# A gated recurrence's inner blocks: full-array matmuls replaced by fp32 matmuls of 32 stationary columns in four strips of PSUM

## The chip, the core and the metric

The kernel runs as one program on one core of a Trainium2 chip. The metric is the time of one execution on the device in microseconds (us). The kernel before has a median of 1879.35 us over 3 runs (1879.05 to 1879.52). TensorE has two clock levels, 1.2 and 2.4 GHz; the profile gives the granted share, and for this kernel it is 1.000.

## The reference, cut to what matters

Two layers of an encoder trunk, each with four branches (sparse attention, retention, a gated recurrence, attention over a memory) between a wide input projection and an output projection. The sequence has 256 positions in chunks of 64, four heads of 128 channels. The change touches the gated recurrence alone:

```
def hgrn2(f, i, q):          # per chunk of 64 positions, per head
    kin = 1.0 - f
    def step(state, inp):
        f_t, k_t, i_t, q_t = inp
        state = f_t[..., None] * state + k_t[..., None] * i_t[..., None, :]
        return state, einsum('bnhd,bnhdv->bnhv', q_t, state)
    ...
```

Unrolled, the output at position t is a sum over earlier positions s of the value i_s times a score: the sum over channels of q_t, kin_s and the product of all gates f between s and t. The kernel computes these scores as matrices of key position by query position, for blocks of 128 x 128 positions, and multiplies them with the values afterwards.

## The kernel before

**The dense work.** TensorE spends nearly all its time on projections (`gemms`, L254). Each fp32 weight is split into a rounded part and a remainder (ScalarE: `whi`, L243; VectorE: `wlo`, L244), and three matmuls (L271 to L273) take the place of one. A weight piece of 256 rows is 12 matmuls of up to 512 moving columns, and is cut four pieces ahead at most (`HL = 4` buffers of each part). All names in rows that begin with `u`, `wo`, `bw`, `mk` and `mv` are such projections.

**The order.** The smaller work of the branches is written as Python generators. After each weight piece `stream.pump` (L127) lets the waiting generators take up to two steps, and what a step issues stands there in each engine's program. `stream.rest(n)` (L106) waits for n pieces and `stream.bank()` (L111) for one of two PSUM tiles. So the order on each engine is fixed when the program is built, and TensorE runs the branch matmuls between projection matmuls.

**The recurrence.** `hgrn_scores` (L553) holds q, kin and the running gate products with channels in partitions and positions along the free axis, 8 groups (4 heads x 2 halves of the sequence) of 128 positions. A score matrix `a` of key positions by query positions is filled from the diagonal outward:

- The diagonal ("own": q times kin) and the positions next to it ("near") are sums over channels: the products are split into two halves (`halves`, L581, an ACT cast and a DVE subtraction for each) and multiplied with a 128 x 128 tile of ones (`summed`, L587; PSUM tiles `cdg` and `cnr`). The sums come out alike in all partitions; a multiplication with an identity and a masked copy take the wanted ones.
- Then three levels, m = 2, 8, 32 (`QUADS`, L615): groups of four blocks of m positions. For each of the 8 groups one fp32 matmul (L637, PSUM tile `cl`) multiplies 128 stationary columns (key positions) with 192 moving columns (the query blocks that are wanted, tile `cV`, made on L624 to L627). Of its output of 128 x 192 only the blocks within each group of four are wanted; masked copies (L642) bring them into `a`. Between the levels `decayed` (L568) multiplies gate products into q and kin.

An fp32 matmul in the program appears in the trace as two passes, each with its own weight load, so `x8` stands for four matmuls. After the levels come the product across the halves (`cx`, L654) and the product with the values (`co`, L528 to L532).

Of the kernel before, what the change touches and what calls it, by code (L numbers as in the profile page):

```python
# [10 lines left out]
F32 = mybir.dt.float32  # L11
F32R = mybir.dt.float32r
U8 = mybir.dt.uint8
# [25 lines left out]
    _o += DM * _n  # L39
assert _o == DM * INW  # L40

C_ID, C_D, C_COS, C_SIN, C_LEV = 0, 128, 128 + 1536, 128 + 1536 + 256, 128 + 1536 + 512
QUADS, FROM = (2, 8, 32), (0, 1, 2, 0, 1, 0)
C_END = C_LEV + 64 + 192 * len(QUADS)


def shape_constants():
    c = np.zeros((128, C_END), np.float32)
    c[:, C_ID:C_ID + 128] = np.eye(128, dtype=np.float32)
    log_g = np.log1p(-np.exp2(-5.0 - np.arange(NH)))  # L50
    t = np.arange(S)
    dist = np.abs(t[None, :] - t[:, None])
    seen = (t[:, None] // CH) <= (t[None, :] // CH)
    dec = np.where(seen[:, None, :], np.exp(log_g[None, :, None] * dist[:, None, :]), 0.0) * ISQ
    c[:, C_D:C_D + 1024] = dec[:128].reshape(128, 1024)
    c[:, C_D + 1024:C_D + 1536] = dec[128:, :, 128:].reshape(128, 512)
    inv = np.float32(10000.0) ** (-np.arange(0, HD, 2, dtype=np.float32) / np.float32(HD))
    ang = t.astype(np.float32)[:, None] * inv[None, :]
    cos, sin = np.cos(ang), np.sin(ang)
    for i in range(2):  # L60
        r = slice(128 * i, 128 * i + 128)
        c[:, C_COS + 128 * i:C_COS + 128 * i + 128] = np.concatenate([cos[r], cos[r]], 1)
        c[:, C_SIN + 128 * i:C_SIN + 128 * i + 128] = np.concatenate([-sin[r], sin[r]], 1)
    s = np.arange(128)
    c[:, C_LEV:C_LEV + 64] = s[:, None] == 2 * np.arange(64)[None, :]
    for i, m in enumerate(QUADS):
        at, block = np.divmod(np.arange(192), 6 * m)
        start = 4 * m * at + m * np.array(FROM)[block // m]
        c[:, C_LEV + 64 + 192 * i:C_LEV + 256 + 192 * i] = (s[:, None] >= start) & (s[:, None] < start + m)
    return c  # L70


# [111 lines left out]
def trunk(ctx: ExitStack, tc: tile.TileContext, x, xt, memt, ng, qkg, hg, lbl, win, wmem, wbr, wout,  # L184
# [23 lines left out]

    xs = cst.tile([128, 2, DM], F32, name="xs")
    csb = cst.tile([128, C_END], F32, name="csb")  # L210
    msb = cst.tile([128, 512 + 192 * len(QUADS)], U8, name="msb")
    ones = cst.tile([128, 128], F32R, name="ones")
# [5 lines left out]
    ident = csb[:, C_ID:C_ID + 128]  # L218
    ve.memset(nhalf, -0.5)

    plan = gemm_plan(wmem, win, wbr, wout)
    stream = Stream()
# [330 lines left out]
    def hgrn_scores(uf, uq, lb, olb, name):  # L553
# [60 lines left out]
        tot = decayed(1, tot)  # L614
        for i, m in enumerate(QUADS):  # L615
            n = 32 // m
            yield
            mask = msb[:, 512 + 192 * i:704 + 192 * i].rearrange("p (n x) -> p n x", n=n)
            vs = []
            for half in range(2):  # L620
                qv = qf[:, 512 * half:512 * half + 512].rearrange("p (n b j) -> p n b j", b=4, j=m)
                dv = tot.rearrange("p (h n b) -> p h n b", h=2, b=4)[:, half]
                vt = G([128, 4 * n, 6, m], f"{name}V{half}")
                ac.copy(vt[:, :, 0:3, :], qv[:, :, 1:4, :])  # L624
                ve.tensor_mul(vt[:, :, 3:5, :], qv[:, :, 2:4, :],
                              dv[:, :, 1:3, None].to_broadcast([128, 4 * n, 2, m]))
                ve.tensor_mul(vt[:, :, 5, :], vt[:, :, 4, :], dv[:, :, 1:2].to_broadcast([128, 4 * n, m]))  # L627
                vs.append(vt.rearrange("p (g n) b j -> p g (n b j)", g=4))
            yield
            yield from stream.rest(1)  # L630
            for half in range(2):
                yield
# [6 lines left out]
                pv = ps[:, :, :192].rearrange("p g (n x) -> p g n x", n=n)  # L639
                av = a[:, 4 * half:4 * half + 4, :].rearrange("p g (n x) -> p g n x", n=n)  # L640
                for t0, at, w in ((1, 0, 3), (2, 3, 2), (3, 5, 1)):
                    ve.copy_predicated(av[:, :, :, t0 * m:],  # L642
                                       mask[:, None, :, at * m:(at + w) * m].to_broadcast([128, 4, n, w * m]),
                                       pv[:, :, :, at * m:(at + w) * m])
                stream.free()
            yield
            tot = decayed(m, tot)
            yield
            tot = decayed(2 * m, tot)
        yield from stream.rest(3)  # L650
        yield from stream.bank()
        ps = PB(name + "x")[:, :512].rearrange("p (h t) -> p h t", h=4)
# [79 lines left out]
    def last_constants():  # L732
        yield from stream.rest(27)
        sy.dma_start(csb[:, C_D:], cf[:, C_D:])
        yield from stream.rest(7)
        po.tensor_copy(msb[:, :512].rearrange("p (g t) -> p g t", g=8),
                       csb[:, C_LEV:C_LEV + 64][:, None, :].to_broadcast([128, 8, 64]))
        po.tensor_copy(msb[:, 512:], csb[:, C_LEV + 64:C_END])
        one = G([128, 128], "one")
        ve.memset(one, 1.0)  # L740
        ac.copy(ones, one)
        lower_bounds()

    lbv = cst.tile([128, L, NH], F32, name="lbv")
# [197 lines left out]
```

## Time and profile before

| | |
|---|---|
| median of 3 runs | 1879.35 us (1879.05 to 1879.52) |
| profiled execution, its own time | 1878.9 us |
| its span, first to last instruction | 1877.1 us |
| TensorE (PE) busy | 1869.4 us, 8574 passes |
| VectorE (DVE) busy | 1153.6 us |
| ScalarE (ACT) busy | 872.8 us |
| GpSimd (POOL) busy | 252.8 us |
| granted TensorE clock | 1.000 |

A pass's busy time in the profile holds its way through the array, which overlaps the next pass. What a pass costs TensorE is the step from its start to the next one's start. `PEld` is TensorE's weight load, which is issued by the same sequencer.

### The profile page before, as it was taken

The page shows a single profiled execution, that of the slowest core. Times are in us where ns is not written, and L with a number is a line of the kernel's source. Part 1 is how long each engine was busy: PE and PEld are TensorE (multiplying, and loading weights), DVE is VectorE, ACT ScalarE, POOL GpSimd, SP SyncE. Part 2 cuts the span into 40 slices and gives each one's busy share as a digit, 9 for nine tenths or more (in the row PEclk, how much of TensorE's full clock was granted, in tenths as well). Part 3 has the DMA queues.
Part 4 walks back from the last instruction along what each step waited for, and adds up shares of the span by engine and source line. Part 5 has one row for each costly group of instructions (what it writes and reads, how often), then busy time and mean ns, then how long its engine had stood idle before and what let it go on. Part 6 is the DMA issues. An engine that isn't in the chain of part 4 may idle for free.

```text
span 1877.1 us, 22921 instructions
## 1 busy us (share of the span) xinstructions
PE 1869.4 (100%) x8574; PEld 1560.4 (83%) x8574; DVE 1153.6 (61%) x1269; ACT 872.8 (46%) x1013; POOL 252.8 (13%) x404
## 2 busy tenths in 40 slices
PE   9999999999999999999999999999999999999999
PEld 7888888888888888888888888888888888888887
DVE  6645788675655555555566578867565555555554
ACT  5654445544444444444455454553444444444442
POOL 0301032241200000000021103224120000000000
PEclk9999999999999999999999999999999999999999
DMA  9865656677756565565686565768765656556563
GB/s 347 287 215 163 218 173 202 215 197 188 218 188 211 190 203 202 185 208 196 199 233 213 168 219 172 207 199 208 194 204 202 197 196 209 187 200 201 189 209 116
DMA packets 165662, 381.39 MB, mean 203 GB/s; under 512 B 111792, under 2 KB 112688, under 8 KB 124720
## 3 DMA queue, kind: packets, MB, share of 16 engines
q1 hardware_dynamic: 153120, 367.86, 60.0%
q0 software_dynamic: 12288, 11.95, 3.7%
q8 instruction: 67, 1.10, 0.3%
q14 instruction: 43, 0.35, 0.1%
q10 hardware_dynamic: 144, 0.13, 0.0%
HBM read 353.92 MB, written 2.10 MB: 190 GB/s over the span
## 4 chain that ended last, share of the span: by engine, by line
PE 98%; DMA 1%; DVE 1%; issue 0%; ACT 0%; SPq 0%; DVEq 0%; ACTq 0%
PE u L271 24%; PE u L272 24%; PE u L273 24%; PE wo L272 3%; PE wo L271 3%; PE bw L273 3%; PE bw L272 3%; PE bw L271 3%; PE wo L273 3%; PE cl L637 1%; DMA raw<-in_wmem 1%; PE mk L273 1%; PE mv L272 1%; PE mv L271 1%; PE mv L273 1%; PE mk L272 1%
## 5 line engine op out<-in xcount | busy, mean ns | idle before, releaser
L244 DVE TENSOR_TENSOR wlo<-raw,whi 128x1024 fp32r<-128x1024 f32 (+2 forms) x676 | 803.6, 1193 | 634.3 <-ACT whi L243 630.4
L243 ACT CAST whi<-raw 128x1024 fp32r<-128x1024 f32 (+2 forms) x676 | 695.6, 1031 | 928.5 <-PE u L273 712.4
L322 POOL DMA_DIRECT2D mgp<-mgpi x64 | 36.8, 583 | 798.8 <-ACT whi L243 503.6
L272 PE MATMUL u<-wlo,x10h 128*128 128x512 f32 (+2 forms) x256 | 98.4, 384 | 0.6 <-DVE wlo L244 0.6
L272 PE MATMUL u<-wlo,x00h 128*128 128x512 f32 (+2 forms) x256 | 98.4, 384 | 0.6 <-DVE wlo L244 0.6
L271 PE MATMUL u<-whi,x03h 128*128 128x512 f32 (+2 forms) x256 | 98.9, 386 | 0.0
L271 PE MATMUL u<-whi,x13h 128*128 128x512 f32 (+2 forms) x256 | 98.9, 386 | 0.0
L271 PE MATMUL u<-whi,x00h 128*128 128x512 f32 (+2 forms) x256 | 98.9, 386 | 0.0
L271 PE MATMUL u<-whi,x10h 128*128 128x512 f32 (+2 forms) x256 | 98.9, 386 | 0.0
L271 PE MATMUL u<-whi,x02h 128*128 128x512 f32 (+2 forms) x256 | 98.8, 386 | 0.0
L271 PE MATMUL u<-whi,x12h 128*128 128x512 f32 (+2 forms) x256 | 98.8, 386 | 0.0
L271 PE MATMUL u<-whi,x01h 128*128 128x512 f32 (+2 forms) x256 | 98.7, 386 | 0.0
L271 PE MATMUL u<-whi,x11h 128*128 128x512 f32 (+2 forms) x256 | 98.7, 386 | 0.0
L272 PE MATMUL u<-wlo,x03h 128*128 128x512 f32 (+2 forms) x256 | 98.2, 383 | 0.0
L272 PE MATMUL u<-wlo,x13h 128*128 128x512 f32 (+2 forms) x256 | 98.2, 383 | 0.0
L272 PE MATMUL u<-wlo,x02h 128*128 128x512 f32 (+2 forms) x256 | 98.2, 383 | 0.0
L272 PE MATMUL u<-wlo,x12h 128*128 128x512 f32 (+2 forms) x256 | 98.2, 383 | 0.0
L272 PE MATMUL u<-wlo,x01h 128*128 128x512 f32 (+2 forms) x256 | 98.2, 383 | 0.0
L272 PE MATMUL u<-wlo,x11h 128*128 128x512 f32 (+2 forms) x256 | 98.2, 383 | 0.0
L273 PE MATMUL u<-whi,x00l 128*128 128x512 f32 (+2 forms) x256 | 98.2, 383 | 0.0
L273 PE MATMUL u<-whi,x01l 128*128 128x512 f32 (+2 forms) x256 | 98.1, 383 | 0.0
L273 PE MATMUL u<-whi,x10l 128*128 128x512 f32 (+2 forms) x256 | 98.1, 383 | 0.0
(390 smaller groups left out, 3715.7 us busy)
## 6 DMA issues: line engine op xcount, KB each, us to landing
raw<-in_win SPq DMA_DIRECT2D x240, 1024.0 KB, 4.9
raw<-in_wbr SPq DMA_DIRECT2D x32, 1024.0 KB, 4.8
raw<-in_wout SPq DMA_DIRECT2D x32, 1024.0 KB, 4.9
raw<-in_wmem SPq DMA_DIRECT2D x14, 1024.0 KB, 8.2
raw<-in_win SPq DMA_DIRECT2D x8, 656.0 KB, 4.0
raw<-in_win SPq DMA_DIRECT2D x8, 512.0 KB, 3.5
raw<-in_wmem SPq DMA_DIRECT2D x8, 256.0 KB, 5.7
xr<-in_xt SPq DMA_DIRECT2D x4, 512.0 KB, 8.2
```

What stands on the lines that cost most here:

```text
L243: ac.copy(hi[:, a:b, :], r)
L244: ve.tensor_sub(lo[:, a:b, :], r, hi[:, a:b, :].bitcast(F32))
L271: te.matmul(ps[:, t, :n], ah[:, 2 * j + k, c], wh[:, k, :], start=first, stop=False)
L272: te.matmul(ps[:, t, :n], ah[:, 2 * j + k, c], wl[:, k, :], start=False, stop=False)
L273: te.matmul(ps[:, t, :n], al[:, 2 * j + k, c], wh[:, k, :], start=False, stop=last)
L322: q.dma_start(whole[b, :, a], inner[a, :, b])
L637: te.matmul(ps[:, g, :192], kd[:, h, (g % 2) * 128:(g % 2) * 128 + 128], vs[half][:, g, :], start=True, stop=True)
```

## The change

Only the 32 x 32 blocks on the diagonal of `a` are computed for the diagonal, the neighbours and the levels 2 and 8. Four matmuls of 32 stationary columns each write their own strip of 32 PSUM partitions, with the moving columns of that strip alone. They collect in a tile `in32` of 128 x 8 x 32 (32 key positions in each strip), which four copies then bring into the zeroed `a`. The sums with ones are plain fp32 matmuls now: `halves` and `summed` are gone, `ones` is an fp32 tile of 32 columns, and the neighbours share the PSUM tile of the diagonal. Level 32 has a part of its own with three strips of 96, 64 and 32 moving columns, whose output is wanted whole and is copied by ACT. The constants shrink accordingly.

```diff
@@ hgrn_scores
-        def halves(x, n, name):
-            hi, lo = G([128, n], name + "h", F32R), G([128, n], name + "l", F32R)
-            ac.copy(hi, x)
-            ve.tensor_sub(lo, x, hi.bitcast(F32))
-            return hi, lo
-
-        def summed(ps, x, c):
-            te.matmul(ps, ones, x[0][:, c:c + 512], start=True, stop=False)
-            te.matmul(ps, ones, x[1][:, c:c + 512], start=False, stop=True)
+        strips = [slice(32 * i, 32 * i + 32) for i in range(4)]
...
-        own = halves(own, 1024, name + "o")
         yield
...
-        near = halves(near, 512, name + "n")
+        a = G([128, 8, 128], name + "A")
+        po.memset(a, 0.0)
         yield from stream.rest(2)
         yield from stream.bank()
         ps = PB(name + "dg")
-        for c in (0, 512):
-            summed(ps[:, c:c + 512], own, c)
-        a = G([128, 8, 128], name + "A")
-        ve.tensor_mul(a, ps.rearrange("p (g t) -> p g t", g=8), ident[:, None, :].to_broadcast([128, 8, 128]))
-        stream.free()
-        yield
-        yield from stream.bank()
-        ps = PB(name + "nr")[:, :512]
-        summed(ps, near, 0)
-        ve.copy_predicated(a.rearrange("p g (b two) -> p (g b) two", two=2)[:, :, 1], msb[:, :512], ps)
+        for i, st in enumerate(strips):
+            te.matmul(ps[st, 0:256].rearrange("p (g t) -> p g t", g=8), ones,
+                      own.rearrange("p (g i t) -> p g i t", g=8, i=4)[:, :, i, :], start=True, stop=True)
+        for i, st in enumerate(strips):
+            te.matmul(ps[st, 512:640].rearrange("p (g t) -> p g t", g=8), ones,
+                      near.rearrange("p (g i t) -> p g i t", g=8, i=4)[:, :, i, :], start=True, stop=True)
+        in32 = G([128, 8, 32], name + "in")
+        ve.tensor_mul(in32, ps[:, 0:256].rearrange("p (g t) -> p g t", g=8), eight(ident, 32))
...
-            yield from stream.rest(1)
-            for half in range(2):
-                yield
-                yield from stream.bank()
-                ps = PB(f"{name}l{i}").rearrange("p (g c) -> p g c", g=4)
-                for g in range(4):
-                    h = 2 * half + g // 2
-                    te.matmul(ps[:, g, :192], kd[:, h, (g % 2) * 128:(g % 2) * 128 + 128], vs[half][:, g, :],
-                              start=True, stop=True)
...
+            yield from stream.rest(2)
+            yield from stream.bank()
+            ps = PB(f"{name}l{i}")[:, :384].rearrange("p (g c) -> p g c", g=8)
+            for g in range(8):
+                for i, st in enumerate(strips):
+                    te.matmul(ps[st, g, :], kd[:, g // 2, (g % 2) * 128 + 32 * i:(g % 2) * 128 + 32 * i + 32],
+                              vs[g // 4][:, g % 4, 48 * i:48 * i + 48], start=True, stop=True)
...
+        yield
+        for st in strips:
+            ve.tensor_copy(a[st, :, st], in32[st])
...
+        yield from stream.rest(2)
+        yield from stream.bank()
+        ps = PB(name + "l2").rearrange("p (g t) -> p g t", g=8)
+        for g in range(8):
+            for i, (c, w) in enumerate(((0, 96), (96, 64), (160, 32))):
+                te.matmul(ps[strips[i], g, 128 - w:], kd[:, g // 2, (g % 2) * 128 + 32 * i:(g % 2) * 128 + 32 * i + 32],
+                          vs[g // 4][:, g % 4, c:c + w], start=True, stop=True)
+        for i, w in enumerate((96, 64, 32)):
+            ac.copy(a[strips[i], :, 128 - w:], ps[strips[i], :, 128 - w:])
+        stream.free()
```

What it moves on TensorE, in the first layer. The sums over channels stand in two places before, with one weight piece between them (a row with `x4` is four matmuls, 128x512 the output's partitions and columns):

```order
889 L273 MATMUL u<-whi,x00l 128x328
890 L588 MATMUL cdg<-coh,ones 128x512
891 L589 MATMUL cdg<-col,ones 128x512
892 L588 MATMUL cdg<-coh,ones 128x512
893 L589 MATMUL cdg<-col,ones 128x512
894 L271 MATMUL u<-whi,x01h 128x328
...
905 L273 MATMUL u<-whi,x01l 128x328
906 L588 MATMUL cnr<-cnh,ones 128x512
907 L589 MATMUL cnr<-cnl,ones 128x512
908 L271 MATMUL u<-whi,x01h 128x328
```

After the change both stand in the first of these places, and the level of m = 2, which was two groups of four matmuls of 128x192, is one group of 32:

```order
889 L274 MATMUL u<-whi,x00l 128x328
890 L599 MATMUL cdg<-cown,ones 32x256 x4
891 L602 MATMUL cdg<-cnear,ones 32x128 x4
892 L272 MATMUL u<-whi,x01h 128x328
...
963 L274 MATMUL u<-whi,x03l 128x328
964 L630 MATMUL cl_1801<-cV_1725,ck 32x48 x16
965 L630 MATMUL cl_1801<-cV_1729,ck 32x48 x16
966 L272 MATMUL u<-whi,x00h 128x512
```

So six interruptions of the projections by full-array groups for the levels become three by strips, and two for the sums become one.

On ScalarE, at the place where the sums over channels are prepared, the kernel before has two casts of `halves` among the casts of weight pieces:

```order
57 L243 CAST whi<-raw 128x512 x4
58 L583 CAST coh<-cown 128x1024
59 L243 CAST whi<-raw 128x656
60 L583 CAST cnh<-cnear 128x512
61 L243 CAST whi<-raw 128x656 x3
62 L346 ACTIVATE qi_1652<-u,rs0r 128x256 x2
63 L243 CAST whi<-raw 128x656 x4
```

After the change the casts of weight pieces stand there alone:

```order
56 L244 CAST whi<-raw 128x512 x4
57 L244 CAST whi<-raw 128x656 x4
58 L347 ACTIVATE qi_1643<-u,rs0r 128x256 x2
59 L244 CAST whi<-raw 128x656 x3
60 L620 COPY cV_1725<-cq 128x64x6
```

The three copies of level 32 come on the same engine later, between casts:

```order
76 L358 ACTIVATE aqsq<-aqu 128x1024
77 L244 CAST whi<-raw 128x1024
78 L663 COPY cA<-cl_2114 32x8x96
79 L663 COPY cA<-cl_2114 32x8x64
80 L663 COPY cA<-cl_2114 32x8x32
81 L244 CAST whi<-raw 128x1024 x5
```

## Rows read from the trace of the kernel before

**Rows 1.** The page: busy times, the chain that ended last, weight casts.

```profile
PE 1869.4 (100%) x8574; PEld 1560.4 (83%) x8574; DVE 1153.6 (61%) x1269; ACT 872.8 (46%) x1013; POOL 252.8 (13%) x404
PE 98%; DMA 1%; DVE 1%; issue 0%; ACT 0%; SPq 0%; DVEq 0%; ACTq 0%
L243 ACT CAST whi<-raw 128x1024 fp32r<-128x1024 f32 (+2 forms) x676 | 695.6, 1031 | 928.5 <-PE u L273 712.4
```

**Rows 2.** Timeline of PE, sums over channels: start, length, line, passes.

```profile
198.31 0.40 PE L588 MATMUL cdg<-coh,ones 128*128 128x512 f32 x1
...
199.25 0.31 PE L271 MATMUL u<-whi,x01h 128*128 128x328 f32 x1
...
201.04 0.41 PE L588 MATMUL cnr<-cnh,ones 128*128 128x512 f32 x1
...
201.51 0.31 PE L271 MATMUL u<-whi,x01h 128*128 128x328 f32 x1
```

**Rows 3.** Timeline of PE around one of the twelve groups of L637.

```profile
213.28 1.46 PE L637 MATMUL cl<-cV,ck 128*128 128x192 f32 x8
...
214.80 0.40 PE L272 MATMUL u<-wlo,x00h 128*128 128x512 f32 x1
```

**Rows 4.** Groups by form on PE: count, busy us, mean ns of one.

```profile
L637 PE MATMUL cl<-cV,ck 128*128 128x192 f32 x96 | 17.5, 325 | 0.0
```

**Rows 5.** Timeline of PE: fp32 passes of 128 and of 256 columns.

```profile
276.88 1.05 PE L654 MATMUL cx<-cq,ck 128*128 128x128 f32 x8
...
278.00 0.40 PE L272 MATMUL u<-wlo,x02h 128*128 128x512 f32 x1
...
440.56 1.89 PE L539 MATMUL bs<-bqpt,bkpt 128*128 128x256 f32 x8
...
442.52 0.40 PE L272 MATMUL u<-wlo,x01h 128*128 128x512 f32 x1
```

**Rows 6.** Timeline of PE: L481, 64-row matmuls that alternate between the array's halves.

```profile
269.89 0.39 PE L273 MATMUL u<-whi,x01l 128*128 128x512 f32 x1
270.20 1.16 PE L481 MATMUL ixrp<-ixkt,ixqt 64*128 64x128 f32 x16
...
271.63 0.39 PE L272 MATMUL u<-wlo,x01h 128*128 128x512 f32 x1
...
302.01 0.39 PE L273 MATMUL u<-whi,x02l 128*128 128x512 f32 x1
302.32 1.13 PE L481 MATMUL ixrp<-ixkt,ixqt 64*128 64x256 f32 x8
...
303.73 0.40 PE L272 MATMUL u<-wlo,x02h 128*128 128x512 f32 x1
```

**Rows 7.** Timeline of PEld: weight loads of L654 beside Rows 5.

```profile
276.65 1.08 PEld L654 LDWEIGHTS cx<-cq,ck 128*128 128x128 f32 x8
```

**Rows 8.** PE's waits, and its timeline ahead of Rows 2.

```profile
PE u L272 <- DVE wlo L244: 1.2, 4, 0.5
193.32 0.31 PE L271 MATMUL u<-whi,x00h 128*128 128x328 f32 x1
...
194.04 0.31 PE L273 MATMUL u<-whi,x00l 128*128 128x328 f32 x1
...
195.39 0.31 PE L273 MATMUL u<-whi,x00l 128*128 128x328 f32 x1
...
196.56 0.42 PE L272 MATMUL u<-wlo,x00h 128*128 128x328 f32 x1 [0.46 <-DVE wlo L244]
196.82 0.31 PE L273 MATMUL u<-whi,x00l 128*128 128x328 f32 x1
```

**Rows 9.** Timeline of ACT in the same stretch.

```profile
190.68 1.05 ACT L583 CAST coh<-cown 128x1024 fp32r<-128x1024 f32 x1 [2.24 <-DVE cown L592]
...
194.37 0.62 ACT L583 CAST cnh<-cnear 128x512 fp32r<-128x512 f32 x1 [2.00 <-DVE cnear L596]
194.90 2.02 ACT L243 CAST whi<-raw 128x656 fp32r<-128x656 f32 x3
```

More of the change, by code (lines that the diff above doesn't have):

```diff
@@ L63, in shape_constants @@
         c[:, C_SIN + 128 * i:C_SIN + 128 * i + 128] = np.concatenate([-sin[r], sin[r]], 1)
-    s = np.arange(128)
-    c[:, C_LEV:C_LEV + 64] = s[:, None] == 2 * np.arange(64)[None, :]
+    c[:, C_LEV:C_LEV + 16] = s[:, None] == 2 * np.arange(16)[None, :]
     for i, m in enumerate(QUADS):
-        at, block = np.divmod(np.arange(192), 6 * m)
+        at, block = np.divmod(np.arange(48), 6 * m)
         start = 4 * m * at + m * np.array(FROM)[block // m]
-        c[:, C_LEV + 64 + 192 * i:C_LEV + 256 + 192 * i] = (s[:, None] >= start) & (s[:, None] < start + m)
+        c[:, C_LEV + 16 + 48 * i:C_LEV + 64 + 48 * i] = (s[:, None] >= start) & (s[:, None] < start + m)
     return c
@@ L601, in hgrn_scores @@
         ps = PB(name + "dg")
-        for c in (0, 512):
-            summed(ps[:, c:c + 512], own, c)
-        a = G([128, 8, 128], name + "A")
-        ve.tensor_mul(a, ps.rearrange("p (g t) -> p g t", g=8), ident[:, None, :].to_broadcast([128, 8, 128]))
-        stream.free()
-        yield
-        yield from stream.bank()
-        ps = PB(name + "nr")[:, :512]
-        summed(ps, near, 0)
-        ve.copy_predicated(a.rearrange("p g (b two) -> p (g b) two", two=2)[:, :, 1], msb[:, :512], ps)
+        for i, st in enumerate(strips):
[6 more added lines that the diff above has]
+        ve.tensor_mul(in32, ps[:, 0:256].rearrange("p (g t) -> p g t", g=8), eight(ident, 32))
+        ve.copy_predicated(in32.rearrange("p g (b two) -> p g b two", two=2)[:, :, :, 1], eight(msb[:, 0:16], 16),
+                           ps[:, 512:640].rearrange("p (g b) -> p g b", g=8))
         stream.free()
@@ L622, in hgrn_scores @@
                 dv = tot.rearrange("p (h n b) -> p h n b", h=2, b=4)[:, half]
-                vt = G([128, 4 * n, 6, m], f"{name}V{half}")
+                vt = G([128, 16 * n, 6, m], f"{name}V{half}")
                 ac.copy(vt[:, :, 0:3, :], qv[:, :, 1:4, :])
                 ve.tensor_mul(vt[:, :, 3:5, :], qv[:, :, 2:4, :],
-                              dv[:, :, 1:3, None].to_broadcast([128, 4 * n, 2, m]))
-                ve.tensor_mul(vt[:, :, 5, :], vt[:, :, 4, :], dv[:, :, 1:2].to_broadcast([128, 4 * n, m]))
+                              dv[:, :, 1:3, None].to_broadcast([128, 16 * n, 2, m]))
@@ L628, in hgrn_scores @@
+                ve.tensor_mul(vt[:, :, 5, :], vt[:, :, 4, :], dv[:, :, 1:2].to_broadcast([128, 16 * n, m]))
                 vs.append(vt.rearrange("p (g n) b j -> p g (n b j)", g=4))
-            yield
-            yield from stream.rest(1)
-            for half in range(2):
-                yield
-                yield from stream.bank()
-                ps = PB(f"{name}l{i}").rearrange("p (g c) -> p g c", g=4)
-                for g in range(4):
-                    h = 2 * half + g // 2
-                    te.matmul(ps[:, g, :192], kd[:, h, (g % 2) * 128:(g % 2) * 128 + 128], vs[half][:, g, :],
-                              start=True, stop=True)
[L639 to L645, printed above, removed]
+            yield from stream.rest(2)
@@ L646, in hgrn_scores @@
+            for t0, at, w in ((1, 0, 3), (2, 3, 2), (3, 5, 1)):
+                ve.copy_predicated(av[:, :, :, t0 * m:], eight(mask[:, :, at * m:(at + w) * m], n, w * m),
+                                   pv[:, :, :, at * m:(at + w) * m])
+            stream.free()
             yield
@@ L649, in hgrn_scores @@
             tot = decayed(2 * m, tot)
+        yield
+        for st in strips:
+            ve.tensor_copy(a[st, :, st], in32[st])
+        vs = []
+        for half in range(2):
+            qv = qf[:, 512 * half:512 * half + 512].rearrange("p (n b j) -> p n b j", b=4, j=32)
+            dv = tot.rearrange("p (h n b) -> p h n b", h=2, b=4)[:, half]
+            vt = G([128, 4, 6, 32], f"{name}V{half}")
+            ac.copy(vt[:, :, 0:4:3, :], qv[:, :, 1:3, :])
+            ac.copy(vt[:, :, 5, :], qv[:, :, 3, :])
+            ve.tensor_mul(vt[:, :, 1:5:3, :], qv[:, :, 2:4, :], dv[:, :, 1:3, None].to_broadcast([128, 4, 2, 32]))
+            ve.tensor_mul(vt[:, :, 2, :], vt[:, :, 4, :], dv[:, :, 1:2].to_broadcast([128, 4, 32]))
+            vs.append(vt.rearrange("p g b j -> p g (b j)"))
+        yield from stream.rest(2)
[7 more added lines that the diff above has]
+            ac.copy(a[strips[i], :, 128 - w:], ps[strips[i], :, 128 - w:])
+        stream.free()
+        yield
+        tot = decayed(32, tot)
+        yield
+        decayed(64, tot)
         yield from stream.rest(3)
@@ L735, in last_constants @@
         yield from stream.rest(7)
[L736 to L741, printed above, removed]
+        po.tensor_copy(msb, csb[:, C_LEV:C_END])
         lower_bounds()
```

24 lines of the change are left out of this document (15 added, 9 removed).

## Prediction

> **What bounds the kernel now.** I read the page first. TensorE is busy for the whole span, 1869.4 of 1877.1 us, and the chain that ended last runs through PE for 98% [rows 1]. The reader is to see that no stage of this kernel waits for something else for long: whatever TensorE is spared shortens the run by that amount, and whatever the change makes it do or wait for is added. So every price below is a step on TensorE, from the start of one pass to the start of the next, and the other engines count only where they make TensorE wait. The granted clock is 1.000 over the span, the 2.4 GHz level.
>
> Next I read the timeline of PE at the places that the change touches. The four passes for the diagonal's sums take 199.25 - 198.31 = 0.94 us, so a step of 512 columns is 0.23 us; the two for the neighbours take 0.47 us [rows 2]. A level's group of eight passes (four fp32 matmuls of 192 columns) starts at 213.28, and the second projection matmul behind it at 214.80; less the 0.23 of the first one, the group costs 1.29 us, or 0.162 a pass [rows 3]. There are 96 such passes, twelve groups, six in each layer [rows 4]. Two other fp32 groups give the price by columns: 128 columns, (278.00 - 276.88 - 0.23)/8 = 0.112 us a pass; 256 columns, (442.52 - 440.56 - 0.23)/8 = 0.216 [rows 5]. That is about 0.81 ns a column and a small constant: by the line through these two, 96 columns take 0.086, 64 take 0.060, 48 take 0.047 and 32 take 0.034. No pass under 128 columns stands in the trace, so these four are estimates.
>
> **What the change removes.** Per layer 0.94 + 0.47 + 6 x 1.29 = 9.15 us of TensorE, 18.3 in both.
>
> **What it adds, if the strips run side by side.** The new matmuls have 32 stationary columns and write four separate strips of PSUM; whether the four run at the same time decides this case. Before has no matmul of this kind. The nearest row is L481, where matmuls of 64 rows alternate between the two halves of the array's rows. Its 16 passes of 128 columns take 271.63 - 269.89 less two projection steps of 0.23, or 1.28 us. Full-array passes would be 16 x 0.112 = 1.79. Its 8 passes of 256 columns take 303.73 - 302.01 - 0.46 = 1.26 us, against 8 x 0.216 = 1.73 [rows 6]. Two passes at a time would be 0.90 and 0.86 us, and what is left is the same in both: 0.38 to 0.40 us. So I read that the two halves run side by side in full, and that going into such a group and out of it costs TensorE 0.40 us. For strips of columns I take the same rule with four in place of two:
>
> - sums over channels: two passes of 256 and two of 128 columns for all four strips, 0.432 + 0.224, and 0.40: 1.06 us
> - levels 2 and 8: for each of 8 groups two passes of 48 columns, 16 x 0.047 = 0.75, and 0.40: 1.15 us each, 2.30 for both
> - level 32: the strip of 96 columns is the longest, 16 x 0.086 = 1.38, and 0.40: 1.78 us
>
> The sum is 5.14 us a layer, 4.01 less than is removed, so 8.0 us for both layers. The bounds of this step: if changing in and out of strips cost nothing, 3.2 us more are won (8 groups x 0.40); with twice that price 3.2 us less. If nothing runs side by side it is the first rival.
>
> **A wait that goes.** PE waits four times for a weight remainder, 1.2 us by the profile's gaps [rows 8], and these lie just ahead of the sums, two in each layer. By steps they cost more than the gaps say. Nine steps from 194.04 to 195.39 show 0.15 as the regular step of 328 columns; from 193.32 to 194.04 there are two steps in 0.72 us, 0.42 late, and from 195.39 to 196.82 three in 1.43, 0.98 late [rows 8]. The cause stands on ACT: the cast of `halves` at 194.37 had made ACT wait 2.00 us for the product on DVE, and three casts of weight pieces stood behind it [rows 9]; the earlier cast at 190.68 had waited 2.24. The change takes both casts and both DVE subtractions away, and ACT's order shows weight casts alone there. I take the whole 1.40 us a layer as won, 2.8 in both; nothing of it is the other bound, since the products themselves still stand on DVE.
>
> **Edits that I cost at nothing.** DVE's masks shrink to a quarter of the columns or half the instructions, and it gains four small copies into `a`. ACT gains three copies from PSUM behind level 32, for which it waits on TensorE, where DVE waited before. Weight casts queue behind them, but ACT mostly waits for TensorE to free weight buffers (712.4 us of its idle time before L243, [rows 1]), and a cast is for a piece that is used three pieces, 3 x 12 x 0.23 = 8.3 us, later. The group of 1.78 us, three copies of together some 2 us (estimated at twice a weight cast of 1.03, [rows 1]), the cast and a subtraction of about its length fit in that; without this cover each us of delay would cost a us, twice. POOL's zeroing of `a` stands behind DMA issues, and POOL is busy 13% of the span [rows 1]. Products and matmul are still two pieces apart (`rest(2)`), or 5.5 us, for a handful of DVE operations, so I expect no new wait for `cV`. The smaller constants are loaded under projections.
>
> **The sum.** 1878.9 of the profiled execution, less 8.0 and 2.8, is 1868.1. The median of before is 0.45 above its profiled execution, so I forecast a median of 1868.5 us, 0.58% less.
>
> **The rivals.**
>
> *The strips take turns, and it gets slower.* Rows 6 show row halves, whose passes read different partitions; strips of columns all read the same 128 partitions, and nothing in this trace shows that these can be streamed four times at once. In turn the layer costs: sums 8 x 0.216 + 8 x 0.112 + 0.40 = 3.02; levels 2 and 8, 64 x 0.047 + 0.40 = 3.41 each; level 32, 16 x (0.086 + 0.060 + 0.034) + 0.40 = 3.28. Together 13.1, or 3.97 more than before; with 2.8 won ahead of the sums, 1879.35 + 7.9 - 2.8 = 1884.5. It decides from the point at which, on average, fewer than 1.3 strips run at a time (11.5 us of columns divided by that, and 1.6 for four groups, reach the 9.15 + 1.4 of before). Slow feeding ends on the same side: the 16 loads and 16 passes at 270.20 lie in 1.16 us, so 0.036 us apiece is the most that issuing one can take [rows 6]; at that price a level of 128 loads and passes takes 4.6 us and level 32 with 96 of them 3.5, the layer 1.06 + 2 x 5.0 + 3.9 = 15.0, and the run 1888.
>
> *In turn, and every load shows.* All strips share the array's rows, and a load might have to wait for the pass in flight above it. A quarter of a full pass of 0.112 us is 0.028 for 32 columns; 192 passes a layer then show 5.4 us on top of 13.1, which gives 1895. Against it speak eight loads of L654, which begin at 276.65, a step ahead of the eight passes that begin at 276.88, and run through in step with them in the same rows of the array [rows 7], [rows 5]. The Trainium skill states this mechanism as a rule ("TensorE: Matmul & The Clock Gate", section "The mechanism"): a weight load overlaps matmuls in flight only where the row groups differ. For the full array the trace does not agree with it, by the loads just named. The same page ("Measured speedup vs the span model") gives 2.38 times for three strips of columns run together, which would make an estimate between the forecast and the next rival; no run here shows it.
>
> *Two at a time.* If the streams of one partition can only be doubled, the columns of the first rival count half: 1.71 for the sums, 1.91 for each of two levels, and for level 32 the strip of 64 columns beside that of 96 and then that of 32 alone, 16 x 0.120 + 0.40 = 2.32. That is 7.85 a layer, 1.30 less than before: 1879.35 - 2.6 - 2.8 = 1874.0.
>
> *Nothing is gained since PE waits anew.* Fewer passes bring projections earlier against the casts. Before, only the four waits above cost TensorE anything in the middle of the run, so weight casts have room, and I give it little.
>
> **How the numbers follow.** Side by side 0.60 (1868.5, between 1865 and 1872 by the bounds of the change of mode and of the wait that goes); two at a time, or between that and side by side, 0.20 (1872 to 1878); in turn or fed too slowly 0.15 (1884 to 1888); every load showing 0.03 (1895); new waits that eat the gain 0.02. What a measurement of this kernel can tell from no change is about 0.2%, 3.8 us. Faster by more holds in the first case and in three quarters of the second, 0.75; within it the rest of the second and the new waits, 0.07; slower 0.18. The range is 1865 to 1878, which leaves out what is slower.
>
> **What would show each step.** The timeline of PE: the strips' groups should take 1.06, 1.15, 1.15 and 1.78 us by the steps, with passes of four strips starting close together; groups near 3 us mean that they take turns. The waits for `wlo` ahead of the sums should be gone from PE's list. The sums should start 1.4 us earlier in the layer, and the next layer about 5.4 us earlier in the span. The forecast is wrong if strips share one stream, if a pass of 48 columns costs far more than 0.047, or if a projection waits for a cast behind the copies of level 32.

## The result and the profile after

The changed kernel has a median of 1869.07 us over 4 runs (1868.33 to 1869.54), beside 1879.2 us for the kernel before on the same chip: a ratio of 0.9945 [0.9932, 0.9957], where 1868.5 us was forecast. The profiled execution took 1868.33 us and its span is 1866.5 us, 10.6 less than before's. Two rows of the page of the changed kernel answer to [rows 1]: busy time of each engine, and the chain that ended last.

```profile
PE 1859.3 (100%) x8850; PEld 1548.4 (83%) x8850; DVE 1138.0 (61%) x1249; ACT 874.8 (47%) x1018; POOL 252.5 (14%) x405
...
PE 98%; DMA 1%; DVE 1%; POOL 0%; ACT 0%; issue 0%; SPq 0%; DVEq 0%; ACTq 0%
```

TensorE has 276 passes more than before and is busy 10.1 us less. It is still busy for the whole span, so the difference can be added up from its steps. The timeline of PE of the changed kernel follows, at the places where the prediction named a price, and at one where it named none (start, length, line, passes in the group; in brackets the idle time ahead and what ended it):

```profile
196.76 0.31 PE L274 MATMUL u<-whi,x00l 128*128 128x328 f32 x1
197.01 0.64 PE L599 MATMUL cdg<-cown,ones 128*32 128x256 f32 x8
...
198.05 0.31 PE L273 MATMUL u<-wlo,x01h 128*128 128x328 f32 x1
...
223.19 0.39 PE L274 MATMUL u<-whi,x02l 128*128 128x512 f32 x1
223.51 0.89 PE L630 MATMUL cl<-cV,ck 128*32 128x48 f32 x64
...
224.66 0.40 PE L273 MATMUL u<-wlo,x02h 128*128 128x512 f32 x1
...
237.83 0.39 PE L274 MATMUL u<-whi,x00l 128*128 128x512 f32 x1
238.15 1.51 PE L660 MATMUL cl<-cV,ck 128*32 128x96 f32 x48
...
239.93 0.40 PE L273 MATMUL u<-wlo,x01h 128*128 128x512 f32 x1
...
280.00 0.39 PE L272 MATMUL u<-whi,x03h 128*128 128x512 f32 x1
281.05 0.50 PE L273 MATMUL u<-wlo,x03h 128*128 128x512 f32 x1 [0.66 <-DVE wlo L245]
281.38 0.40 PE L274 MATMUL u<-whi,x03l 128*128 128x512 f32 x1
```

A group is priced as the prediction did it with [rows 6]: from the start of the last projection ahead of it to the second one behind it, less two projection steps. The sums take 198.05 - 196.76 - 2 x 0.15 = 0.99 us. A level of 64 passes takes 224.66 - 223.19 - 0.46 = 1.01 us (1.02 as a mean over the four such levels), and level 32 takes 239.93 - 237.83 - 0.46 = 1.64. That is 0.99 + 2 x 1.02 + 1.64 = 4.67 us a layer where 5.14 were forecast. The reader is to see the 64 passes of one level inside 0.89 us: one pass each 0.014 us, where a pass of 48 columns alone was estimated at 0.047. They can't have run one after the other. The starts of the single passes in the trace say it directly: the four strips' passes of one round start 0.007 us apart, and the next round starts 0.0425 us behind the one before it.

The steps ahead of the sums are regular now, 0.15 each from 195.71 to 196.76, and the list of PE's waits of the changed kernel has none there; it begins so (total, times, longest):

```profile
PE heat L692 <- DVE warm L689: 1.1, 1, 1.1
PE u L273 <- DVE wlo L245: 0.7, 1, 0.7
```

The four waits of [rows 8] are gone, but one new wait for a weight remainder stands in the second row. It is that of 281.05. By steps it makes TensorE 281.38 - 280.00 - 0.46 = 0.92 us late, and the same place in the second layer costs 0.27 by the same two steps, too little for the list. Together that is 1.2 us that the prediction did not have.

The timeline of ACT of the changed kernel shows both why the old waits went and that the new copies do no harm:

```profile
190.62 0.74 ACT L244 CAST whi<-raw 128x656 fp32r<-128x656 f32 x1 [0.70 <-PE u L274]
...
239.78 1.76 ACT L663 COPY cA<-cl 32x768 f32<-32x768 f32 x3 [2.66 <-PE cl L660]
241.55 2.14 ACT L244 CAST whi<-raw 128x1024 fp32r<-128x1024 f32 x2
```

At 190.62 ACT waits for TensorE to free a buffer, which is its usual state, where before it had stood 2.24 and 2.00 us for the products on DVE [rows 9]. Behind level 32 the copies take 1.76 us, near the estimated 2, after ACT had been idle for 2.66; two casts follow at once, and no wait of PE answers to them.

The balance of the span: 9.15 us a layer were to go and 9.22 did (the mean over all its groups in both layers), 4.67 came, so 2 x 4.55 = 9.1 us less. The waits ahead of the sums give 2.8, the new lateness takes 1.2. That makes 10.7, and the span is 10.6 us shorter.

Single spans also hold what TensorE loses at the start of the run, where it waits for the first weights of the memory's keys; over the profiles of this case that list entry (`mk`, for ACT's cast `whi`) lies between none and 1.5 us. So a second measure is used below: the time from the first projection of the input (`u`) to the last pass of TensorE. In the changed kernel these are

```profile
94.75 0.39 PE L272 MATMUL u<-whi,x00h 128*128 128x512 f32 x1
...
1861.52 0.39 PE L274 MATMUL wo<-whi,mg3l 128*128 128x512 f32 x1
```

so this stretch takes 1766.77 us. In the kernel before it takes 1777.32, 10.6 more, and in a second profile of the changed kernel, on another chip, again 1766.77.

### The profile page after: what moved, and what is told of

It reads as the page before. It is cut to its first block, busy times and chain, and to the rows that moved or that the text cites. A ratio compares the mean times of both kernels' runs of the same rounds, so it can differ in the third digit from the quotient of the medians.

```text
span 1866.5 us, 23415 instructions
## 1 busy us (share of the span) xinstructions
PE 1859.3 (100%) x8850; PEld 1548.4 (83%) x8850; DVE 1138.0 (61%) x1249; ACT 874.8 (47%) x1018; POOL 252.5 (14%) x405
## 4 chain that ended last, share of the span: by engine, by line
PE 98%; DMA 1%; DVE 1%; POOL 0%; ACT 0%; issue 0%; SPq 0%; DVEq 0%; ACTq 0%
PE u L272 24%; PE u L273 24%; PE u L274 24%; PE wo L272 3%; PE wo L273 3%; PE bw L274 3%; PE bw L273 3%; PE bw L272 3%; PE wo L274 3%; DMA raw<-in_wmem 1%; PE mk L274 1%; PE mv L274 1%; PE mv L272 1%; PE mv L273 1%; PE mk L272 1%; PE mk L273 1%
## 5 line engine op out<-in xcount | busy, mean ns | idle before, releaser
L274 PE MATMUL u<-whi,x12l 128*128 128x512 f32 (+2 forms) x256 | 98.2, 383 | 0.0
L274 PE MATMUL u<-whi,x02l 128*128 128x512 f32 (+2 forms) x256 | 98.2, 383 | 0.0
L274 PE MATMUL u<-whi,x13l 128*128 128x512 f32 (+2 forms) x256 | 98.2, 383 | 0.0
L274 PE MATMUL u<-whi,x03l 128*128 128x512 f32 (+2 forms) x256 | 98.2, 383 | 0.0
```

Source lines behind the costliest of these rows:

```text
L274: te.matmul(ps[:, t, :n], al[:, 2 * j + k, c], wh[:, k, :], start=False, stop=last)
```

## The experiments

The two theories after the result: the four strips run side by side whatever their order, and what a group costs besides its longest strip is a price for going into strips and out of them; or what was seen hangs on the order in which strips are fed, on the number of instructions, or on something else in the group. Each of the first four runs moves one of these.

**Strips in turn.** The two loops of the levels 2 and 8 are exchanged, so that one strip gets its 16 passes before the next:

```diff
-            for g in range(8):
-                for i, st in enumerate(strips):
+            for i, st in enumerate(strips):
+                for g in range(8):
```

> The changed kernel with the two loops of levels 2 and 8 exchanged: all 8 groups of one strip, then the next strip, so 16 passes of one strip stand together. In the changed kernel such a level costs 1.02 us of TensorE (steps from start to start) and the run 1869.1. Theory: four strips run side by side only since the program brings them in turn and TensorE looks a few instructions ahead; strip by strip they go almost one after another, 64 x 0.0425 + 0.34 = 3.06 us a level, four levels in the two layers, so about 8 us slower, near 1877. Rival: each strip has a queue of its own that holds 16 passes, and the order does not matter: 1.02 us a level, no change.

Measured: 1874.72 us over 7 runs (1874.44 to 1875.19), 0.9972 [0.9961, 0.9982] of before. Timeline of PE of this kernel around one level:

```profile
224.66 0.39 PE L274 MATMUL u<-whi,x02l 128*128 128x512 f32 x1
224.98 2.49 PE L630 MATMUL cl<-cV,ck 128*32 128x48 f32 x64
...
227.74 0.39 PE L273 MATMUL u<-wlo,x02h 128*128 128x512 f32 x1
```

A level takes 227.74 - 224.66 - 0.46 = 2.62 us in place of 1.02. In four levels that is 6.4 us, and the span is 6.4 us longer than that of the changed kernel (1872.9). Neither end was met: wholly in turn would be 64 x 0.0425 + 0.34 = 3.06 us, side by side 1.02 (the two prices are those of the split level, below). (2.62 - 0.34)/0.0425 is 53.6 passes one after another in place of 64, or some 3.4 saved at each of the three changes of strip. The starts of the single passes show how: a strip's passes start 0.0425 us apart; the next strip's first pass starts 0.006 us behind the thirteenth of the sixteen, so that four passes of the old strip still run beside the new one; and the new strip's second pass starts 0.067 us behind its first, not 0.0425. So strips run side by side only where their passes stand near each other in the program.

**Turns of four groups.** The test of that reading: each strip gets 8 passes in a turn, so there are 7 changes.

```diff
-            for g in range(8):
-                for i, st in enumerate(strips):
+            for gs in (range(0, 4), range(4, 8)):
+                for i, st in enumerate(strips):
+                    for g in gs:
```

> The changed kernel in which levels 2 and 8 bring four groups (eight passes) of one strip, then four of the next, and so twice through the four strips. Strip by strip with sixteen passes in a row cost 2.62 us, and there a strip began when four passes of the one before it were left. Theory: four passes of a strip can wait while TensorE takes in the next strip's; then a strip begins four passes after the one before it, the second turn 16 passes after the first, 36 x 0.0425 + 0.34 = 1.87 us a level. Rivals: the price falls with the length of the turn to that of the changed kernel, 1.02 us; or any turn longer than one matmul costs 2.62.

Measured: 1873.93 us in one run (before 1879.9 on that chip). Timeline of PE:

```profile
225.67 0.39 PE L274 MATMUL u<-whi,x02l 128*128 128x512 f32 x1
225.98 1.93 PE L631 MATMUL cl<-cV,ck 128*32 128x48 f32 x64
...
228.18 0.39 PE L273 MATMUL u<-wlo,x02h 128*128 128x512 f32 x1
```

A level takes 2.05 us (2.06 as a mean), where 1.87 was expected; the two other cases, 1.02 and 2.62, are out. (2.06 - 0.34)/0.0425 = 40.5 passes: the last 8 and 7 changes of 4.6, so again 8 - 4.6 = 3.4 passes are saved at a change. The starts show that the reading holds as it was set down: the next strip begins beside the fifth of the eight passes, with four left, as in the first run. What the expectation left out is the price of a change, 0.006 us and the first step of 0.067 in place of 0.0425, together 0.031: 7 x 0.031 = 0.22 us, which brings 1.87 within 0.03 of the measured 2.06.

**Levels twice.** Each matmul of the levels 2 and 8 is issued twice, with the same result:

```diff
-            for g in range(8):
+            for g in 2 * list(range(8)):
```

> The changed kernel with every matmul of levels 2 and 8 issued twice (same result). Theory: four strips side by side at 0.0425 us a pass, and a fixed 0.34 us for going into strips and out of them: a level goes from 1.02 to 1.70 us, 2.7 us in four levels, near 1871.8. Rivals: the price is in issuing, all of it by the number of instructions: 2.04 us a level, 4.1 us in all; or strips in turn: 2.7 us more a level, 10.9 in all.

Measured: 1871.97 us over 4 runs (1871.08 to 1872.78), 0.9957 [0.9942, 0.9972] of before. Timeline of PE of this kernel, inside one doubled level in the first layer and around another in the second:

```profile
209.65 1.55 PE L630 MATMUL cl<-cV,ck 128*32 128x48 f32 x125
211.74 0.28 PE L630 MATMUL cl<-cV,ck 128*32 128x48 f32 x3 [0.54 <-issue]
...
1110.72 0.39 PE L274 MATMUL u<-whi,x12l 128*128 128x512 f32 x1
1111.04 1.63 PE L630 MATMUL cl<-cV,ck 128*32 128x48 f32 x128
...
1112.93 0.40 PE L273 MATMUL u<-wlo,x12h 128*128 128x512 f32 x1
```

The undisturbed level takes 1112.93 - 1110.72 - 0.46 = 1.75 us, and three of the four 1.70 to 1.78, where 1.70 was expected. So 64 more passes cost 0.7 us, or 16 rounds of four at some 0.045, and not the whole 1.02 again, nor the 2.7 of passes in turn. The fourth level has a hole of 0.54 us ahead of its last three passes, for which the profile shows nothing that PE waited for; it takes 2.49. The profiled execution is the longest of the four runs, so the hole need not be in the others. Its cause stays open.

**Levels in four pieces.** The level's 8 groups are issued two at a time, with a weight piece between them:

```diff
             for g in range(8):
+                if g in (2, 4, 6):
+                    yield from stream.rest(1)
```

> The changed kernel with each of levels 2 and 8 cut into four pieces of two groups, with a weight piece of projections between them. Theory: 0.34 us is paid each time that TensorE goes into strips and out of them: three more times in each of four levels, 12 x 0.34 = 4.1 us, and a piece costs 0.17 + 0.34 = 0.51 us; near 1873.2. Rival: the fixed part is a wait at a level's start alone, and pieces cost 0.17 us after the first: no change.

Measured: 1871.84 us over 4 runs (1871.64 to 1872.52), 0.9956 [0.9939, 0.9972] of before. Timeline of PE around one of the sixteen pieces:

```profile
236.26 0.39 PE L274 MATMUL u<-whi,x00l 128*128 128x512 f32 x1
236.58 0.38 PE L632 MATMUL cl<-cV,ck 128*32 128x48 f32 x16
...
237.23 0.40 PE L273 MATMUL u<-wlo,x00h 128*128 128x512 f32 x1
```

A piece takes 237.23 - 236.26 - 0.46 = 0.51 us, as expected. Four pieces cost 2.05 and the whole level 1.02, with the same 64 passes; so the fixed price is (2.05 - 1.02)/3 = 0.34 us, and a round of four strips (1.02 - 0.34)/16 = 0.0425. In the changed kernel's trace the 0.34 us falls in four places around a level: 0.09 ahead of the first pass, 0.02 in the first round, 0.11 between the last round and the next projection, and 0.11 in that projection's own step.

By steps the pieces cost 4.1 us more in all. The new lateness of 1.2 us is gone in this kernel: its list of PE's waits has no row of `u` (the recurrence's tail comes six weight pieces later here). That leaves 2.9, and the medians differ by 2.8. But from the first `u` to the last pass this kernel takes 1770.6 us, 3.8 more than the changed kernel, so the agreement of the medians is in part chance. The other 0.9 us lies in the projection steps between the pieces, many of which are some 5 to 14 ns longer here. By this measure the twelve further groups cost (3.8 + 1.2)/12 = 0.42 us each, so 0.34 is the price of a group's own steps and not all of it in this kernel; in the changed kernel the balance above leaves about 0.1 us for such a rest. Why the steps between the pieces are longer stays open.

**The casts put back.** The changed kernel with both casts and subtractions of `halves`, their results unused:

```diff
+        halves(own, 1024, name + "o")
         yield
...
+        halves(near, 512, name + "n")
         a = G([128, 8, 128], name + "A")
```

> The changed kernel with the two casts on ACT and the two subtractions on DVE of the former split put back where they stood, their results unused. Theory: the two waits of TensorE for weight remainders ahead of the sums, 1.40 us a layer in the kernel before, came from ACT waiting for the products in front of weight casts; they return, 2.8 us in all, near 1871.9. Rival: these waits came from elsewhere (the other matmuls, the PSUM tile), and the time stays at 1869.1.

Measured: 1870.77 us over 4 runs (1870.48 to 1871.71), 0.9951 [0.9936, 0.9966] of before. PE's waits of this kernel and a part of its timeline ahead of the sums:

```profile
PE u L273 <- DVE wlo L245: 1.9, 5, 0.7
```

```profile
195.37 0.41 PE L272 MATMUL u<-whi,x00h 128*128 128x328 f32 x1
196.24 0.42 PE L273 MATMUL u<-wlo,x00h 128*128 128x328 f32 x1 [0.46 <-DVE wlo L245]
196.50 0.31 PE L274 MATMUL u<-whi,x00l 128*128 128x328 f32 x1
```

The four old waits are back beside the new one, with the same longest gap of 0.46 as in [rows 8]; by steps they cost 2.79 us, the 2.8 of the prediction, and the prices of the strips' groups are unchanged. The span is 2.4 us longer than the changed kernel's, the median 1.7, and the stretch from the first `u` to the last pass 2.6.

**The sums alone, in the kernel before.** Before without `halves`: fp32 matmuls with a 128 x 128 tile of ones, the rest untouched.

```diff
-            te.matmul(ps, ones, x[0][:, c:c + 512], start=True, stop=False)
-            te.matmul(ps, ones, x[1][:, c:c + 512], start=False, stop=True)
+            te.matmul(ps, ones, x[:, c:c + 512], start=True, stop=True)
```

> The kernel before with the split taken away alone: the sums over channels as plain fp32 matmuls with 128 x 128 ones, no casts and no subtractions; full-array matmuls everywhere. Theory: the two waits a layer for weight remainders go (2.8 us won in both layers), and the sums cost six passes of 512 columns at 0.43 us in place of six at 0.23, 2.58 us a layer against 1.41 (2.3 us lost): 0.5 us faster than before, no change that a measurement can tell. Rival: the waits stay, and it is 2.3 us slower.

Measured: 1878.9 us over 11 runs (1878.3 to 1880.9), 0.9997 [0.9989, 1.0006] of before. Timeline of PE of this kernel around the diagonal's sums:

```profile
196.86 0.31 PE L273 MATMUL u<-whi,x00l 128*128 128x328 f32 x1
197.01 1.88 PE L582 MATMUL cdg<-cown,ones 128*128 128x512 f32 x4
...
198.88 0.31 PE L272 MATMUL u<-wlo,x01h 128*128 128x328 f32 x1
```

These sums take 198.88 - 196.86 - 0.30 = 1.72 us and the neighbours' 0.86, 2.58 in place of the 1.41 of [rows 2]: two layers pay 2.3 us more, win the 2.8 of the waits (the list of PE's waits has no row of `u` here), and the run stays where it was. So dropping the halves pays only together with the strips, which bring the sums to 0.99.

**The new wait: ACT or DVE.** The timeline of DVE of the changed kernel ahead of 281.05:

```profile
273.81 1.22 DVE L245 TENSOR_TENSOR wlo<-raw,whi 128x1024 fp32r<-128x1024 f32 x1
274.95 0.28 DVE L490 TENSOR_SCALAR ixsc<-ixrl,ixw 128x128 f32<-128x128 f32 x1
275.26 2.67 DVE L492 SCALAR_TENSOR_TENSOR ixsc<-ixrl,ixw,ixsc 128x128 f32<-128x128 f32 x7
...
278.64 1.25 DVE L317 STREAM_TRANSPOSE akpti<-aku 128x1024 f32<-128x1024 f32 x1 [0.52 <-DMA cnpt<-cnpti]
279.81 1.18 DVE L245 TENSOR_TENSOR wlo<-raw,whi 128x1024 fp32r<-128x1024 f32 x1
```

and that of the kernel before, at the same operations:

```profile
272.80 2.68 DVE L491 SCALAR_TENSOR_TENSOR ixsc<-ixrl,ixw,ixsc 128x128 f32<-128x128 f32 x7
...
276.66 1.21 DVE L244 TENSOR_TENSOR wlo<-raw,whi 128x1024 fp32r<-128x1024 f32 x1
...
278.38 1.23 DVE L316 STREAM_TRANSPOSE akpti<-aku 128x1024 f32<-128x1024 f32 x1
```

Before, a weight remainder stood between the index scores (`ixsc`) and the transposition of the keys (`akpti`). After, no remainder is begun between 273.81 and 279.81. Which operations stand together is decided by how the generators fall between weight pieces, and the recurrence now needs fewer of these. DVE also stood idle for 0.52 us there, for the transfer of a tile of the recurrence's tail (`cnpt`). But ACT has a wait at that place too, a scaling that by the profile waits 3.03 us for the same transfer, with casts behind it:

```profile
278.85 1.16 ACT L368 ACTIVATE aqpt<-aqpt,qks 128x1024 f32<-128x1024 f32 x1 [3.03 <-DMA cnpt<-cnpti]
```

The first experiment moves that scaling alone:

```diff
             pt = yield from transposed(u, name + "pt")
+            if name == "aq":
+                yield from stream.rest(3)
             ac.activation(pt, pt
...
```

> The changed kernel, in which ACT's scaling of the transposed queries of the sparse attention is issued three weight pieces later. In the changed kernel this instruction waits 3.0 us (first layer) for DMA moves, in front of weight casts, and two projections start late behind it: 0.93 us in the first layer and 0.27 in the second. Theory: these go, 1.2 us in all, near 1867.9. Rival: the projections wait for DVE, which itself waits at that time, and the lateness stays.

Measured: 1868.84 us over 5 runs (1868.29 to 1869.25), 0.9942 [0.9929, 0.9954] of before. Timeline of PE:

```profile
280.86 0.39 PE L272 MATMUL u<-whi,x03h 128*128 128x512 f32 x1
281.91 0.50 PE L273 MATMUL u<-wlo,x03h 128*128 128x512 f32 x1 [0.66 <-DVE wlo L245]
282.25 0.40 PE L274 MATMUL u<-whi,x03l 128*128 128x512 f32 x1
```

The gap is the same 0.66 us, the lateness over both layers the same 1.2, and the stretch from the first `u` to the last pass is 1766.82 us, as in the changed kernel. The theory that ACT's scaling makes the remainder late fell. The second experiment moves the recurrence's tail six weight pieces back, with DVE's part of it:

```diff
         decayed(64, tot)
-        yield from stream.rest(3)
+        yield from stream.rest(9)
         yield from stream.bank()
```

> The changed kernel in which the recurrence's tail (product across the halves, product with the values, norm) waits nine weight pieces after the last level in place of three, as late as in the kernel before. Theory: the new lateness of projections in the changed kernel (1.2 us) came from DVE's order, in which eight score operations of the attention's selection and the transposition of its keys fell between the same two weight pieces (4.9 us on DVE) since the recurrence's earlier tail moved them; with the later tail they stand between different pieces as before, the lateness goes, near 1867.7. Rival: it comes with the earlier selection whatever the tail does, and stays.

Measured: 1868.02 us over 5 runs (1867.35 to 1869.37), 0.9936 [0.9922, 0.995] of before. Timeline of DVE of this kernel at the transposition:

```profile
273.03 1.21 DVE L245 TENSOR_TENSOR wlo<-raw,whi 128x1024 fp32r<-128x1024 f32 x1
...
275.15 1.25 DVE L317 STREAM_TRANSPOSE akpti<-aku 128x1024 f32<-128x1024 f32 x1 [0.32 <-issue]
276.32 2.32 DVE L245 TENSOR_TENSOR wlo<-raw,whi 128x1024 fp32r<-128x1024 f32 x2
```

The pause between two remainders is 276.32 - 274.24 = 2.1 us now, where it was 279.81 - 275.03 = 4.8, and TensorE is nowhere late in this stretch. So it is what stands on DVE between two remainders that makes the new wait. This run takes away both the order and the 0.52 us of waiting for `cnpt` in it, and doesn't tell how much of the lateness each of them made.

The span of the profiled execution shows no gain (1867.6). It lost 2.3 us up to the first `u`, at 97.03 in place of 94.75: TensorE waited for the first cast of the memory's keys for 1.4 us, and then, from 12 to 15 us, the granted clock was 0.50, the level of 1.2 GHz, with steps of 0.43 us where they are 0.23. From the first `u` to the last pass it takes 1765.5 us, 1.2 less than the changed kernel, as the theory had it.

**Even strips at level 32.** The 96 columns of the first strip are halved over strips 0 and 3, so that the longest has 64; ACT copies four blocks in place of three. First on top of the run with the moved scaling, then on top of the later tail:

```diff
+LAST = ((0, 0, 0, 32, 48), (1, 1, 96, 64, 64), (2, 2, 160, 96, 32), (3, 0, 48, 80, 48))
...
-            for i, (c, w) in enumerate(((0, 96), (96, 64), (160, 32))):
+            for i, j, c, t, w in LAST:
```

> As the kernel with the later scaling, and in level 32 the 96 columns of the first strip are halved, the second half on the fourth strip, which is idle there: the longest strip has 64 columns. Theory: level 32 costs 16 x 0.055 + 0.34 = 1.23 us in place of 1.64, 0.8 us less in both layers on top of 1.2: near 1867.1. Rival: a fourth strip costs as much in issuing as it saves in columns, and level 32 stays at 1.64.

Measured: 1867.9 us over 5 runs (1867.47 to 1868.19), 0.9937 [0.9923, 0.995] of before; level 32 takes 1.22 us, and the new lateness stays. The forecast added the 1.2 us of the moved scaling, which did not come. The stretch from the first `u` to the last pass is 1765.92 us, 0.85 under the changed kernel's.

> The later tail together with the even strips of level 32 (longest strip 64 columns, 1.22 us in place of 1.64 in the run before). Theory: 1.2 us and 0.84 us add up: near 1866.8, 0.1% under the changed kernel. Rival: one of them is given back elsewhere, and it stays at or above 1867.9.

Measured: 1867.15 us over 5 runs (1866.31 to 1867.73), 0.9931 [0.9919, 0.9944] of before. Timeline of PE around level 32:

```profile
238.70 0.39 PE L275 MATMUL u<-whi,x00l 128*128 128x512 f32 x1
239.02 1.09 PE L661 MATMUL cl<-cV,ck 128*32 128x48 f32 x64
...
240.37 0.40 PE L274 MATMUL u<-wlo,x01h 128*128 128x512 f32 x1
```

240.37 - 238.70 - 0.46 is 1.21 us where it was 1.64: with 16 passes more, the group is shorter by what its longest strip is shorter. This is the best version, by steps 0.8 + 1.2 = 2.0 us under the changed kernel. By the times it is 0.1% under it, with overlapping intervals, so that the times alone don't show it. The stretch from the first `u` to the last pass does: 1764.7 us, 2.1 less.

**The changed kernel once more**, on the chip of the runs with the moved scaling, the plain sums and the first even strips:

> The changed kernel itself, beside the three others on the same chip: 1869.1, and by every theory 1.2 us above the first of them and 2.0 above the third.

Measured: 1868.79 us over 5 runs (1868.6 to 1869.42), 0.9942 [0.993, 0.9955] of before, the same result on another chip. The moved scaling, at 1868.84, is not 1.2 us under it: the theory of that run fell.

## Why the prediction was right

**Strips side by side: right, and shown.** A round of four strips costs 0.0425 us (from the split level, and by the starts of the passes), no more than the 0.047 that the prediction estimated for one pass of 48 columns. The doubled level and the even strips price it the same way. "The strips take turns", "every load shows" and "two at a time" would have made a level 3.41, more than that, and 1.91 us; it took 1.02. Order is the condition that the prediction did not name: with strips in turn in the program, a level takes 2.62. The Trainium skill says in "TensorE: Matmul & The Clock Gate", section "The mechanism", that a weight load overlaps matmuls in flight only where the row groups differ; the same section also lets loads go ahead that are meant for a background weight buffer. Here all strips use the same rows, and the 64 loads of a level with their 64 passes took 1.02 us; the trace does not agree with the rule of the row groups taken alone, and no run shows whether such a buffer is the reason. The same page of the Trainium skill has 2.38 times for three strips ("Measured speedup vs the span model"). Four strips of 48 columns here, by 64 x 0.0425 = 2.72 us in turn, run four times as fast without the fixed price, and 2.72/1.02 = 2.7 times as fast when that price is counted on their side; no run has the page's case of three equal strips.

**Two terms were mis-sized, both too dear.** The price of going into strips and out was put at 0.40 us after [rows 6] and is 0.34 by the group's own steps. The pass of 48 columns was put at 0.047 and is 0.0425, that of 96 at 0.086 and is (1.64 - 0.34)/16 = 0.081 (its passes start 0.0825 apart in the trace); the line through the full-array passes [rows 5] held a small constant per pass, of which less is left in strips. Together they made the layer 5.14 where it was 4.67, and the saving 8.0 where it was 9.1.

**The wait that goes: right to a tenth or two.** 2.8 forecast; with the casts put back 2.79 returned by steps and 2.6 from the first `u` to the last pass, and with the casts taken from the kernel before all four waits went. The sums began 198.31 - 197.01 = 1.30 us earlier, where 1.4 was forecast; the first pass in strips starts 0.24 us behind the projection ahead of it, the full-array pass of before 0.15, and that is the other 0.1. The second layer's first `u` came 4.96 us earlier, at 978.58 in place of 983.54, where 5.4 was forecast: 4.55 and 1.4, less the lateness of 0.92.

**The step that failed: edits costed at nothing.** The prediction looked at what the edited lines put on ACT and DVE, and that part held: the copies of level 32 took 1.76 us and held up nobody, and there is no new wait for `cV`. A new wait for weights stood only in its last rival, with a chance of 0.02, and its sum has no term for one. It did not look at what an earlier end of the recurrence does to operations that the diff does not touch. On DVE two pieces of the attention's work lost the remainder that had stood between them, and TensorE is late by 1.2 us. That mishap and the two dear terms nearly cancel: +1.2 beside -1.1. That the median came out within 0.6 us is luck; that it fell where strips side by side put it, and far from the other rivals, is not. The part that is argued and not shown is why the generators fall in this way; shown is only that moving the tail by six pieces undoes it, and that moving ACT's scaling does not.

## What to carry to other kernels

Small fp32 matmuls of 32 stationary columns cost a fixed price per group and then the time of their longest strip: keep strips of equal length, issue them in alternation, and put many in one group. Where TensorE is the bound, count what every group costs from projection to projection. When a change makes one of several interleaved streams shorter, read the new order of the engines that prepare the next weights, also where the diff does not touch them.

## What was not expected of the hardware

- The order of strips decides whether they overlap: alternating 1.02 us, turns of 8 passes 2.06, turns of 16 passes 2.62, with the same 64 passes. In both of the latter the next strip begins when four passes of the one before it are left, and its first pass takes 0.067 us to the second in place of 0.0425.
- The fixed price of a group of strips is 0.34 us by the group's own steps, for 16 passes as for 64, a little less than the 0.38 to 0.40 of the row halves [rows 6]; with the slightly longer projection steps between the pieces of the split level it came to 0.42.
- In one doubled level of 128 matmul passes, PE stood still for 0.54 us ahead of the last three, with nothing in the profile that it waited for; the three other doubled levels have no such hole.
